# The last second product of a two-layer kernel: another order of its products, four sums on GpSimd, a bank put back with the earlier part, two outputs stored in pieces

## The chip, the core and the metric

The kernel runs on one core of a Trainium2 chip. The metric is the device time of one execution in microseconds (us). TensorE (PE) multiplies matrices into PSUM banks; VectorE (DVE) and ScalarE (ACT) take results out of PSUM; GpSimd (POOL) and SyncE (SP) issue most of the DMAs, GpSimd those that add to what lies in memory.

## The reference

```python
x: (16, 512, 768)   w1: (768, 3072)   b1: (3072,)   w2: (3072, 768)   # float32
y = np.matmul(x, w1) + b1
y = np.maximum(y, 0)
return np.matmul(y, w2).astype(np.float32)
```

## The kernel before

The 8192 rows are taken in eight blocks of 1024, the 3072 hidden columns in two chunks of 1536. An iteration is one block with one chunk, so there are 16: eight with the first chunk, then eight with the second. Each iteration has a first product (x by w1, bias and relu, into `y`) and a second (`y` by w2). The operands are fp16, the sums fp32.

**Fewer products.** Both products are cut into blocks and done by a fast scheme: sums of input blocks are formed on VectorE (for the second product the "y sums", L1046), fewer block products are done on TensorE (26 in the second product), and the outputs are formed from sums of products. The tables `SECOND_U`, `SECOND_V` (inputs of each product), `SECOND_CHAINS` and `SECOND_OPS` say how. A chain is a pair of PSUM banks: products ("m") are added into it one after another, and between them an operation ("t") reads the state of the bank pair. An operation gives an output (`out`, with the number of one of eight output blocks of 256 rows by 384 columns), a sum to keep (`sum`, in one of nine slots of `s`), or a value that seeds another chain's banks (`seed`). An operation without a kept sum as second input goes to ScalarE, one with such an input to VectorE (`operation`, L1219, through `combine`, L1207). One product is six matmuls of 128x384: two row halves (j = 0, 1), each over three parts of the hidden columns (`product`, L1196).

**The order of the work.** `SECOND_ORDER` and, for the last iteration, `LAST_ORDER` give the order of the products. All else is a graph of tasks: `Graph.add` records each task with its engine, an assumed duration, its inputs and outputs, and `Graph.run` plans the order of each engine's instructions and which bank or slot a task takes, by due times counted back from TensorE. The engines then run their instructions in that fixed order, each waiting on semaphores. SP and GpSimd issue the stores in their own planned order; an issue waits in its queue for its data, and those behind it wait too.

**The last iteration.** In the second chunk's other iterations GpSimd's stores (L1252, L1255) add the outputs to the first chunk's part, which lies in memory. In the last one, seven of the eight output blocks (`LAST_DIRECT`, all but operation 6) are done without that: SP loads the first chunk's part (`add_priors`, L1174) into places of `x` that are free by then, and it is added on the chip before a plain store from SP (L1250). `prior(to)` is that part of output `to`. Where the operation has a kept sum as well, `prior_task` first adds the kept sum to the part (L1260, x<-x,s, on VectorE since `LAST_POOL` is empty): for operations 0, 1, 3, 4, 5 and 7. Then one VectorE sum of bank and part (L1216) gives the output.

For operation 5 (`LAST_FOLD`) it is otherwise: its part is added into the bank pair on VectorE (`fold`, L1277) before the chain's last product, and ScalarE then copies the finished bank out (L1210). The last output (operation 1, output 3) is formed in two row halves on VectorE (`half`), stored from ACT's and SP's queues (`store_half`, L1245).

The last products are, in this order, 21, 11, 25, 23, 7, 16, 5, 6, 22, 9, 24, 20. Product 22 ends the chain of operation 10, which ScalarE writes, with the sign turned, into the bank pair of product 24; operation 0 (output 2) reads that after product 24. Product 9 leads to operation 5 (output 1), 20 to operation 1 (output 3), 6 to operation 3 (output 5), 5 to operation 2 (output 4), 16 to operation 4 (output 0), 25 to operation 7 (output 7). The kept sums that operations 0, 1, 3, 4, 5 need are those of operations 9, 14, 12, 11 and 20.

At the end of the program every engine loads a flag (L1387) that says whether the inputs were in range for the fast path, branches over the general path (L1512), and SP works off closing semaphores (L1540).

Of the kernel before, what the change touches and what calls it, by code (L numbers as in the profile page):

```python
# [87 lines left out]
SECOND_OPS = {  # L88
    0: (1, 1, 9, 1, 'out', 2, None),
    1: (4, 1, 14, 1, 'out', 3, None),  # L90
    2: (0, 1, None, None, 'out', 4, None),
    3: (4, -1, 12, 1, 'out', 5, None),
    4: (2, -1, 11, 1, 'out', 0, None),
    5: (2, 1, 20, 1, 'out', 1, None),
    6: (3, 1, 19, 1, 'out', 6, None),
    7: (5, 1, 16, 1, 'out', 7, None),
# [19 lines left out]
SECOND_CHAINS = ((('m', 5), ('t', 2)), (('m', 24), ('t', 0)), (('m', 13), ('t', 24), ('m', 4),  # L116
# [6 lines left out]
SECOND_SEEDS = (8, 10, None, 23, 24, 18, 13, None)  # L123
SECOND_ORDER = (13, 15, 4, 17, 10, 8, 12, 18, 3, 0, 1, 14, 2, 19, 23, 21, 11, 16, 25, 22, 7, 9, 6,
    24, 5, 20)
LAST_ORDER = (13, 15, 4, 17, 10, 8, 12, 18, 3, 0, 1, 14, 2, 19, 21, 11, 25, 23, 7, 16, 5, 6, 22,
    9, 24, 20)
LAST_FOLD = (5,)
LAST_DIRECT = (0, 1, 2, 3, 4, 5, 7)
LAST_POOL = ()  # L130

X_FUSE = (3,)
Y_FUSE = (8, 12, 18, 20)
# [453 lines left out]
class Fast:  # L587
# [590 lines left out]
    def add_second(self, it):  # L1178
        c = it // self.NSB
        nc = self.nc  # L1180
        final = it == self.NIT - 1
# [4 lines left out]
        bank, kept, done = {}, {}, 0  # L1186
        uses = [SECOND_OPS[t][2] for t in SECOND_OPS]
        NH, QM = self.NH, self.QM
        steps = sequence(SECOND_CHAINS, SECOND_SEEDS, SECOND_OPS, order)
        last = [n for k, n in steps if k == "t" and SECOND_OPS[n][4] == "out"][-1]  # L1190

        def pair(reg):
            a = reg.at[0]
            return self.ps[:, a:a + 2, 0:NH]

        def product(p, ch, start):  # L1196
            for j, h in ((j, h) for j in range(2) for h in range(3)):
                m0 = h * QM + j * P
                nc.tensor.matmul(self.ps[:, bank[ch].at[j], 0:NH],  # L1199
                                 lhsT=self.y[:, ys[SECOND_U[p]], m0:m0 + P],  # L1200
                                 rhs=self.v2[:, slot[SECOND_V[p]], h, :],
                                 start=(start and h == 0), stop=(h == 2), skip_group_check=True)
# [4 lines left out]
        def combine(engine, out, ps, a, s, b):  # L1207
            if s is None:
                if engine is nc.scalar:
                    nc.scalar.activation(out=out, in_=ps, func=ACTF.Copy, scale=float(a))  # L1210
                else:
                    engine.tensor_scalar(out=out, in0=ps, scalar1=float(a), scalar2=None,
                                         op0=ALU.mult)
                return
            in0, in1 = (ps, s) if a > 0 else (s, ps)
            engine.tensor_tensor(out=out, in0=in0, in1=in1,  # L1216
                                 op=ALU.add if a == b else ALU.subtract)
# [16 lines left out]
                combine(nc.scalar if alone else nc.vector, out, ps, a,  # L1234
                        None if alone else sum_of(kept[u]), b)

        def half(t, j, dest):
            ch, a, _, _, _, to, _ = SECOND_OPS[t]
            out = self.s[:, dest.at[0], 0:NH]
            combine(nc.scalar if t in folds and j == 0 else nc.vector, out, pair(bank[ch])[:, j],  # L1240
                    a, None if t in folds else self.prior(to)[:, j], 1)

        def store_half(to, j, dest):
            s = self.s[:, dest.at[0], 0:NH]
            (nc.scalar, nc.sync)[j].dma_start(out=self.rows_of(it, to)[:, j], in_=s)  # L1245

        def store(to, reg, plain):
            out, rows = sum_of(reg), self.rows_of(it, to)
# [14 lines left out]
        def prior_task(t):  # L1263
            _, _, u, b, _, to, _ = SECOND_OPS[t]
            e, ns = ("POOL", 1850) if t in LAST_POOL else ("DVE", 955)
            self.g.add(e, ns, lambda: add_prior(to, u, b, e),
                       reads=self.prior_keys(to) + [kept[u]], writes=self.prior_keys(to))
# [13 lines left out]

        where = {p: ch for ch, chain in enumerate(SECOND_CHAINS) for k, p in chain if k == "m"}
        folds = set()
        for kind, n in steps:
            if kind == "m":
                self.add_y_sums(order, done)
                done += 1
                ch = where[n]
                start = ch not in bank
                if start:  # L1290
                    bank[ch] = Reg("ps", 2, leaves=1)
                t = SECOND_CHAINS[ch][-1][1]
                if final and t in LAST_FOLD and t in LAST_DIRECT and not start and SECOND_CHAINS[ch][-2] == ("m", n):
                    fold(t)
                    folds.add(t)
                u, w = ys[SECOND_U[n]], slot[SECOND_V[n]]
                self.g.add("PE", 976, lambda p=n, ch=ch, start=start: product(p, ch, start),
                           reads=self.y_keys(u) + [("w2", w, h) for h in range(3)] +
                           ([] if start else [bank[ch]]), writes=[bank[ch]])
                continue  # L1300
            ch, a, u, b, what, to, _ = SECOND_OPS[n]
            reads = [bank[ch]]
            engine = "ACT" if u is None else "DVE"
            if u is not None:
                uses.remove(u)
            if what == "out":
                dest = Reg("s")
                direct = final and n in LAST_DIRECT
                if n in folds:
                    engine = "ACT"  # L1310
                elif direct:
                    engine = "DVE"
                    if u is not None:
                        prior_task(n)
                    reads += self.prior_keys(to)
                elif n in apart:
                    assert b == 1
                    self.g.add("POOL" if c else "SP", 1375 if c else 100,
                               lambda to=to, u=u: store_sum(to, u), reads=[kept[u]],
                               writes=[("out", self.block(it), to)], lat=9.0,  # L1320
                               dma=2.45 if c else 1.2)
                    engine = "ACT"
                elif u is not None:
                    reads.append(kept[u])
                    dest = dest if u in uses else kept[u]
            else:
                if u is not None:
                    reads.append(kept[u])
                if what == "sum":
                    dest = kept[n] = Reg("s") if u is None or u in uses else kept[u]  # L1330
                else:
                    dest = bank[to] = Reg("ps", 2, seeded=1, leaves=1)
            if what == "out" and final and n == last:
                for j in range(2):
                    dest = Reg("s")
                    e = "ACT" if n in folds and j == 0 else "DVE"
                    self.g.add(e, 500, lambda t=n, j=j, dest=dest: half(t, j, dest),
                               reads=reads, writes=[dest])
                    self.g.add(("ACT", "SP")[j], 100, lambda to=to, j=j, dest=dest: store_half(to, j, dest),
                               reads=[dest], writes=[("half", j)], lat=3.5, dma=0.6)  # L1340
                continue
            writes = [dest]
            split = engine == "ACT" and n in HALVES and n not in folds
            self.g.add(engine, 850 if split else 810 if engine == "ACT" else 955,
                       lambda t=n, dest=dest: operation(t, dest), reads=reads, writes=writes,
                       early=0.37 if split else 0)
            if what == "out":
                plain = c == 0 and n not in apart or direct
                self.g.add("SP" if plain else "POOL", 100 if plain else 1375,
                           lambda to=to, dest=dest, plain=plain: store(to, dest, plain),  # L1350
                           reads=[dest], writes=[("out", self.block(it), to)],
                           lat=3.5 if direct else 9.0, dma=1.2 if plain else 2.45)

# [189 lines left out]
```

## Time and profile before

| what | us |
|---|---|
| median of 3 runs (848.92 to 849.01) | 849.0 |
| span of the profiled execution, first to last instruction | 847.4 |
| TensorE busy | 839.4 |
| VectorE busy | 737.9 |
| ScalarE busy | 569.4 |
| GpSimd busy | 164.1 |

The median is the metric; the span belongs to one profiled execution, and the difference of 1.6 us lies around it. Durations in the prediction come from that execution. In a timeline row stand start, duration, engine, line, operation, output <- input, shape and count; a merged row gives the start of the first and the time to the end of the last. In a row of groups, after the bar, stand the busy time in us, the mean of one in ns, and after the next bar the engine's idle time before them with what ended it. "PEld" is TensorE's weight load; an engine's name with a q (SPq) is its queue, where it issues DMAs or works on semaphores. In rows of stretches the busy times of PE, PEld, DVE, ACT and POOL are followed by the granted clock of TensorE, the busy share of the DMA engines and their GB/s.

### The profile page before, as it was taken

To read this page: it belongs to the slowest core of one execution; us is meant where nothing else is said; L and a number is where in the kernel's file an instruction comes from. 1 tells how busy PE (TensorE), PEld (TensorE's weight loads), DVE (VectorE), ACT (ScalarE), POOL (GpSimd) and SP (SyncE) were. 2 spreads that over 40 slices of the span, in tenths; PEclk is the share of its full clock that TensorE was granted. 3 is DMA by queue.
4 is the path that set the end of the run, shared out by engine and by line. 5 is a ranking of instruction groups with operands and counts; after the bars stand their busy time and mean duration, and the time that the engine had idled before them with its cause. 6 is when DMAs were issued, how large, how long until landed. Compare 5 with 4: busy or idle time off the path is not lost. (4 is left out here: it accounts for less than half of the span.)

```text
span 847.4 us, 16784 instructions
## 1 busy us (share of the span) xinstructions
PE 839.4 (99%) x6381; PEld 625.5 (74%) x6381; DVE 737.9 (87%) x1231; ACT 569.4 (67%) x1203; POOL 164.1 (19%) x179
## 2 busy tenths in 40 slices
PE   8999999999999999999999999999999999999997
PEld 7558778686786867768687686877868678686874
DVE  5898987969889697998999979798896979979788
ACT  5866876778677695756858558766757666456463
POOL 5210011102111010010030503224041230501300
PEclk9999999999999999999999999999999999999999
DMA  9996497978988678594793977979789797985836
GB/s 213 202 180 176 81 233 105 163 183 133 222 113 148 169 126 192 95 223 150 224 187 65 192 123 124 187 106 178 125 128 150 116 173 113 147 134 75 146 117 169
DMA packets 170967, 128.93 MB, mean 152 GB/s; under 512 B 93804, under 2 KB 169348, under 8 KB 170884
## 3 DMA queue, kind: packets, MB, share of 16 engines
q0 software_dynamic: 56560, 68.82, 53.1%
q1 hardware_dynamic: 113856, 58.02, 28.3%
q8 instruction: 50, 0.82, 0.4%
q10 hardware_dynamic: 468, 1.00, 0.3%
q14 instruction: 33, 0.27, 0.1%
HBM read 73.54 MB, written 69.21 MB: 168 GB/s over the span
## 5 line engine op out<-in xcount | busy, mean ns | idle before, releaser
L1199 PE MATMUL ps<-v,y 128*128 128x384 f16 x2496 | 408.4, 326 | 0.0
L1073 PE MATMUL ps<-x,v 128*128 128x256 f16 x3600 | 395.7, 273 | 0.0
L1073 PEld LDWEIGHTS <-v 128*128 128x128 f16 x3600 | 352.2, 98 | 42.4 <-issue 0.2
L1199 PEld LDWEIGHTS <-y 128*128 128x128 f16 x2496 | 244.2, 98 | 160.0 <-issue 0.2
L1210 ACT ACTIVATE s<-ps 128x384 f32<-128x384 f32 (+1 forms) x244 | 153.0, 646 | 121.3 <-PE ps L1199 120.2
L1046 DVE TENSOR_TENSOR y<-y 128x768 f16<-128x768 f16 (+1 forms) x384 | 219.4, 619 | 2.6
L1116 DVE CUSTOM_DVE_ANT_0 y<-ps,s 128x512 f16<-128x512 f32 x240 | 156.0, 686 | 54.4 <-ACT s L1113 41.4
L1252 POOL DMA_DIRECT2D out_dram<-s x78 | 93.9, 1470 | 145.4 <-ACT s L1210 97.0
L1113 ACT ACTIVATE s<-ps,bt 128x256 f32<-128x256 f32 x180 | 75.3, 470 | 62.5 <-PE ps L1073 56.7
L828 DVE TENSOR_TENSOR x<-x 128x768 f16<-128x768 f16 (+1 forms) x210 | 113.7, 579 | 1.3
L1113 ACT ACTIVATE y<-ps,bt 128x256 f16<-128x256 f32 x180 | 69.5, 486 | 10.8 <-PE ps L1073 10.8
L1210 ACT ACTIVATE ps<-ps 128x384 f32<-128x384 f32 (+1 forms) x144 | 67.9, 509 | 8.1 <-PE ps L1199 6.6
L1216 DVE TENSOR_TENSOR s<-ps,s 128x768 f32<-128x768 f32 x74 | 70.5, 953 | 1.2 <-issue 0.3
L706 POOL DMA_DIRECT2D xn<-in_x_dram x30 | 25.9, 863 | 214.0 <-DMA x<-xn 99.5
L1216 DVE TENSOR_TENSOR s<-s,ps 128x768 f32<-128x768 f32 x60 | 57.1, 951 | 2.2 <-DVE s L1216 0.5
L767 ACT ACTIVATE junk<-xn 128x768 f16<-128x768 f16 x64 | 54.0, 843 | 0.3
L1255 POOL DMA_DIRECT2D out_dram<-s x15 | 17.7, 1181 | 169.5 <-ACT s L1210 157.7
L1113 ACT ACTIVATE ps<-ps,bt 128x256 f32<-128x256 f32 x60 | 26.7, 445 | 32.4 <-PE ps L1073 31.4
L1109 ACT ACTIVATE ps<-ps 128x512 f32<-128x512 f32 x60 | 35.3, 588 | 4.1 <-DVE y L1116 3.5
L1124 DVE TENSOR_TENSOR s<-s,ps 128x512 f32<-128x512 f32 x30 | 20.6, 688 | 17.7 <-PE ps L1073 17.7
L983 PE MATMUL ps<-x,v 128*128 128x256 f16 (+1 forms) x216 | 32.0, 308 | 0.7 <-DVE x L933 0.7
L1119 DVE SCALAR_TENSOR_TENSOR s<-ps,bt,s 128x256 f32<-128x256 f32 x60 | 26.1, 477 | 4.4 <-PE ps L1073 4.4
(60 smaller groups left out, 304.8 us busy)
## 6 DMA issues: line engine op xcount, KB each, us to landing
out_dram<-s POOLq DMA_DIRECT2D x93, 384.0 KB, 8.8
out_dram<-s SPq DMA_DIRECT2D x70, 384.0 KB, 6.6
xn<-in_x_dram POOLq DMA_DIRECT2D x28, 768.0 KB, 9.7
x<-out_dram SPq DMA_DIRECT2D x7, 384.0 KB, 3.5
v<-in_w_dram POOLq DMA_DIRECT2D x6, 384.0 KB, 10.6
v<-in_w_dram POOLq DMA_DIRECT2D x12, 192.0 KB, 9.1
w1d<-in_w_dram POOLq DMA_DIRECT2D x6, 384.0 KB, 6.5
w2d<-in_w_dram POOLq DMA_DIRECT2D x12, 192.0 KB, 4.9
```

Of the source, the lines that this page charges most:

```text
L767: self.nc.scalar.activation(out=self.junk, in_=self.xn[:, s, :], func=ACTF.Square, accum_out=self.stat[:, self.stat_at["x"] + i:][:, 0:1])
L828: self.nc.vector.tensor_tensor(out=self.two(x, out), in0=self.two(x, in0), in1=self.two(x, in1), op=ALU.add if sign > 0 else ALU.subtract)
L983: nc.tensor.matmul(self.ps[:, ps.at[0], cols], lhsT=self.v1[:, gi, 2 * h + k2, k, j * P:(j + 1) * P], rhs=rhs, start=(k2 == 0 and k == 0), ...
L1046: self.nc.vector.tensor_tensor(out=self.two(self.y, out), in0=self.two(self.y, in0), in1=self.two(self.y, in1), op=ALU.add if sign > 0 els ...
L1073: nc.tensor.matmul(self.ps[:, at, j * self.QM:(j + 1) * self.QM], lhsT=self.v1[:, gi, self.w1s[c][gi][FIRST_V[p]], k, j * P:(j + 1) * P], ...
L1109: nc.scalar.activation(out=out, in_=ps, scale=float(a), func=func if kind == "out" else ACTF.Copy)
L1113: nc.scalar.activation(out=out[:, j], in_=ps[:, j], func=func, scale=float(a), bias=beta(j))
L1116: nc.vector._custom_dve(TENSOR_ADD_SAT, out=out, in0=ps, in1=s, s0=F_MAX, s1=0.0)
L1199: nc.tensor.matmul(self.ps[:, bank[ch].at[j], 0:NH], lhsT=self.y[:, ys[SECOND_U[p]], m0:m0 + P], rhs=self.v2[:, slot[SECOND_V[p]], h, :], ...
L1210: nc.scalar.activation(out=out, in_=ps, func=ACTF.Copy, scale=float(a))
L1216: engine.tensor_tensor(out=out, in0=in0, in1=in1, op=ALU.add if a == b else ALU.subtract)
L1252: nc.gpsimd.dma_start(out=rows, in_=out, accum_op=ALU.add)
```

## The change

It touches the last iteration's second product alone.

- `LAST_ORDER` ends in 21, 11, 23, 25, 7, 16, 5, 6, 9, 22, 20, 24: product 23 comes ahead of 25, 9 ahead of 22, 20 ahead of 24.
- `LAST_POOL` puts the sum of kept sum and first chunk's part on GpSimd for operations 1, 3, 4 and 5. VectorE keeps those of operations 0 and 7. In GpSimd's order the one of operation 5 stands before the adding store of output 6, and those of operations 1, 4 and 3 (outputs 3, 0, 5) behind it.
- `LAST_FOLD` is empty: operation 5 is formed on VectorE from bank and part, as the others are.
- `LAST_TAKE`: the seed of operation 10 is written by VectorE in two row halves as part minus bank, with the first chunk's part (and kept sum) of output 2 already in it. Product 24, now the last, is added to that, so that its bank then holds the finished output 2.
- The last product is issued as two tasks, one for each row half.
- `LAST_PARTS`: output 2 goes out in three pieces: row half 0 (384 columns) copied by ScalarE and stored from SP; of row half 1 the first 192 columns by VectorE, stored from SP, and the rest by ScalarE, stored from ACT's queue.
- `LAST_HALVES`: output 3 (operation 1) is formed in two row halves on VectorE, both stored from SP.

```diff
-LAST_ORDER = (13, 15, 4, 17, 10, 8, 12, 18, 3, 0, 1, 14, 2, 19, 21, 11, 25, 23, 7, 16, 5, 6, 22,
-    9, 24, 20)
-LAST_FOLD = (5,)
+LAST_ORDER = (13, 15, 4, 17, 10, 8, 12, 18, 3, 0, 1, 14, 2, 19, 21, 11, 23, 25, 7, 16, 5, 6, 9,
+    22, 20, 24)
+LAST_FOLD = ()
+LAST_TAKE = {10: 0}
+LAST_HALVES = (1,)
+LAST_PARTS = ((0, 0, 384, "ACT", "SP"), (1, 0, 192, "DVE", "SP"), (1, 192, 384, "ACT", "ACT"))
 LAST_DIRECT = (0, 1, 2, 3, 4, 5, 7)
-LAST_POOL = ()
+LAST_POOL = (1, 3, 4, 5)
...
-        def product(p, ch, start):
-            for j, h in ((j, h) for j in range(2) for h in range(3)):
+        def product(p, ch, start, rows=(0, 1)):
+            for j, h in ((j, h) for j in rows for h in range(3)):
...
+        def part(t, j, cols, dest, e):
+            ch, a = SECOND_OPS[t][:2]
+            combine(nc.scalar if e == "ACT" else nc.vector, self.s[:, dest.at[0], cols],
+                    pair(bank[ch])[:, j, cols], a, None, None)
+
+        def store_part(to, j, cols, dest, e):
+            (nc.scalar if e == "ACT" else nc.sync).dma_start(
+                out=self.rows_of(it, to)[:, j, cols], in_=self.s[:, dest.at[0], cols])
...
+                if final and t == last and SECOND_CHAINS[ch][-2] == ("m", n):
+                    for j in range(2):
+                        self.g.add("PE", 488, lambda p=n, ch=ch, start=start, j=j:
+                                   product(p, ch, start, (j,)),
+                                   reads=self.y_keys(u) + [("w2", w, h) for h in range(3)] +
+                                   ([] if start else [bank[ch]]) +
+                                   ([("taken", t, j)] if t in taken_by else []),
+                                   writes=[("last", j)] + ([] if t in taken_by else [bank[ch]]))
+                    continue
...
             if what == "out" and final and n == last:
+                assert n in folds
+                for j, c0, c1, e, q in LAST_PARTS:
+                    dest = Reg("s")
+                    cols = slice(c0, c1)
+                    self.g.add(e, 100 + 1.05 * (c1 - c0),
+                               lambda t=n, j=j, cols=cols, dest=dest, e=e:
+                               part(t, j, cols, dest, e),
+                               reads=[("last", j)] + (reads if j else []), writes=[dest])
+                    self.g.add(q, 100, lambda to=to, j=j, cols=cols, dest=dest, q=q:
+                               store_part(to, j, cols, dest, q),
+                               reads=[dest], writes=[("part", j, c0)], lat=3.5, dma=0.545 * (c1 - c0) / 384)
+                continue
+            taken = LAST_TAKE.get(n) if final else None
+            if taken is not None:
...
+                folds.add(taken)
+                prior_task(taken)
+                of = SECOND_OPS[taken][5]
+                for j in range(2):
+                    self.g.add("DVE", 548, lambda ch=ch, a=a, of=of, dest=dest, j=j: combine(
+                        nc.vector, pair(dest)[:, j], pair(bank[ch])[:, j], a,
+                        self.prior(of)[:, j], 1),
+                        reads=reads + self.prior_keys(of) + ([dest] if j else []),
+                        writes=[("taken", taken, j)] + ([] if j else [dest]))
+                continue
+            if what == "out" and direct and n in LAST_HALVES:
...
                 for j in range(2):
                     dest = Reg("s")
+                    self.g.add("DVE", 548, lambda j=j, to=to, ch=ch, a=a, dest=dest: combine(
+                        nc.vector, self.s[:, dest.at[0], 0:NH], pair(bank[ch])[:, j], a,
+                        self.prior(to)[:, j], 1), reads=reads, writes=[dest])
+                    self.g.add("SP", 100, lambda to=to, j=j, dest=dest: store_part(
+                        to, j, slice(0, NH), dest, "SP"),
+                        reads=[dest], writes=[("half", to, j)], lat=3.5, dma=0.545)
                 continue
```

More of the change, by code (lines that the diff above doesn't have):

```diff
@@ L1235, in operation @@
                         None if alone else sum_of(kept[u]), b)
[L1237 to L1245, printed above, removed]
+        def part(t, j, cols, dest, e):
[5 more added lines that the diff above has]
+                out=self.rows_of(it, to)[:, j, cols], in_=self.s[:, dest.at[0], cols])
         def store(to, reg, plain):
@@ L1283, in add_second @@
         folds = set()
+        taken_by = set(LAST_TAKE.values()) if final else ()
         for kind, n in steps:
@@ new lines, in add_second @@
+                continue
+            taken = LAST_TAKE.get(n) if final else None
+            if taken is not None:
+                assert engine == "ACT" and what == "seed" and SECOND_OPS[taken][1] == 1
+                folds.add(taken)
[8 more added lines that the diff above has]
+                continue
@@ L1334, in add_second @@
+            if what == "out" and direct and n in LAST_HALVES:
+                assert n not in folds
                 for j in range(2):
                     dest = Reg("s")
[L1336 to L1340, printed above, removed]
+                    self.g.add("DVE", 548, lambda j=j, to=to, ch=ch, a=a, dest=dest: combine(
[4 more added lines that the diff above has]
+                        reads=[dest], writes=[("half", to, j)], lat=3.5, dma=0.545)
@@ L1351, in add_second @@
                            reads=[dest], writes=[("out", self.block(it), to)],
-                           lat=3.5 if direct else 9.0, dma=1.2 if plain else 2.45)
+                           lat=3.5 if direct else 9.0,
+                           dma=1.09 if direct else 1.2 if plain else 2.45)
     def add_check(self):
```

## The prediction

> **What bounds the kernel now.** I read the page's busy shares first, then the groups of the last second product (816.7 us to the end), then its timeline, then the DMA shares of the last 5 us, then SP's last issues.
>
> ```profile
> span 847.4 us, 16784 instructions
> PE 839.4 (99%) x6381; PEld 625.5 (74%) x6381; DVE 737.9 (87%) x1231; ACT 569.4 (67%) x1203; POOL 164.1 (19%) x179
> ```
>
> TensorE is busy 99% of the span, and the change leaves its matmuls as they are: 156 in this last product. So the change can gain only two things: TensorE's waits inside the last product, and the time from TensorE's last matmul to the end.
>
> ```profile
> 816.78 25.66 PE L1199 MATMUL ps<-v,y 128*128 128x384 f16 x156
> 832.47 9.59 PEld L1199 LDWEIGHTS <-y 128*128 128x128 f16 x59 [0.15 <-issue]
> 840.99 1.46 PE L1199 MATMUL ps<-v,y 128*128 128x384 f16 x8
> ```
>
> 156 matmuls in 25.66 us at 326 ns modelled for one start every 0.163 us; eight undisturbed ones start every (1.46 - 0.326)/7 = 0.162. So hardly more than 0.2 us of waiting exists here, and the weight loads show 0.15 of it at 832.47. One product (six matmuls) takes 0.98, and its bank is read about 0.2 after its slot ends. The last matmul ends at 816.78 + 25.66 = 842.44 by the model, so the last slot ends at 842.44 - 0.326 + 0.163 = 842.28.
>
> ```profile
> 837.44 0.96 DVE L1277 TENSOR_TENSOR ps<-ps,x 128x768 f32<-128x768 f32 x1
> 838.31 0.95 DVE L1216 TENSOR_TENSOR s<-ps,x 128x768 f32<-128x768 f32 x1
> 839.17 0.94 DVE L1216 TENSOR_TENSOR s<-x,ps 128x768 f32<-128x768 f32 x1
> 839.49 0.80 ACT L1210 ACTIVATE ps<-ps 128x768 f32<-128x768 f32 x1 [3.42 <-PE ps L1199]
> 840.03 1.82 DVE L1260 TENSOR_TENSOR x<-x,s 128x768 f32<-128x768 f32 x2
> 840.47 0.81 ACT L1210 ACTIVATE s<-ps 128x768 f32<-128x768 f32 x1 [0.18 <-PE ps L1199]
> 841.77 1.88 DVE L1216 TENSOR_TENSOR s<-ps,x 128x768 f32<-128x768 f32 x3
> 843.26 0.38 ACTq L1245 DMA_DIRECT2D out_dram<-s  x1
> 843.68 0.34 SPq L1245 DMA_DIRECT2D out_dram<-s  x1
> ```
>
> VectorE runs without a hole to 843.65: sums of 768 columns start 0.87 apart (837.44, 838.31, 839.17). Its last three (one whole output, two halves) could have started on the last bank at 842.28 + 0.2 = 842.48; the first half starts at 841.77 + 0.87 = 842.64, 0.16 late. So VectorE is only just the last engine. The last store is issued at 843.68, 0.03 after the last half.
>
> ```profile
> 844.50:845.00 0.50, 0.00 (x0) 0.00 (x0) 0.00 (x0) 0.00 (x0) 0.00 (x0) 1.00 1.06 378
> 845.00:845.50 0.50, 0.00 (x0) 0.00 (x0) 0.00 (x0) 0.00 (x0) 0.00 (x0) 0.72 1.01 360
> 845.50:846.00 0.50, 0.00 (x0) 0.00 (x0) 0.00 (x0) 0.00 (x0) 0.00 (x0) 0.50 0.72 250
> ```
>
> (the last columns are the share of the DMA engines' time and GB/s), and of the half stores, the flag's load and the closing instructions:
>
> ```profile
> DMA to landing us min/median/max: 2.5/2.6/2.6
> ...
> L1387 SPq TENSOR_LOAD <-flag x1: 973/973/973, 844.1 to 844.1; - x1
> ...
> L1540 SPq EVENT_SEMAPHORE  x14: 17/28/28, 845.4 to 847.4; - x14
> ```
>
> After that issue two things run side by side. The DMA engines are full (shares about 1) at some 365 GB/s until 845.9, and the last store lands at 843.68 + 2.6 = 846.3. SP, right behind its issue, loads the flag (844.1, 0.97 us) and works off the closing semaphores from 845.4 to 847.4. Either way the end stands 847.4 - 843.68 = 3.7 us behind **SP's last issue**. That issue is the quantity to forecast.
>
> **The change part by part.** The built instruction order shows nothing changed on any engine before this last product.
>
> *Order of products.* 23 goes ahead of 25, 9 ahead of 22, 20 ahead of 24. This spaces out a product and the seed put into its bank, so the waits seen above (0.15, of at most 0.2) should go. Taken: 0.15, so the last slot ends at 842.13. Bounds: 0.2 gained, or 0.15 kept because another bank is late.
>
> *VectorE.* Its removed work: four sums of the first chunk's part and the adding into a bank:
>
> ```profile
> L1260 DVE TENSOR_TENSOR x<-x,s 128x768 f32<-128x768 f32 x6 | 5.5, 951 | 0.0
> L1210 ACT ACTIVATE s<-ps 128x384 f32<-128x384 f32 x8 | 3.8, 495 | 3.3 <-PE ps L1199 3.3
> ...
> L1216 DVE TENSOR_TENSOR s<-ps,x 128x384 f32<-128x384 f32 x2 | 1.0, 548 | 0.0
> ```
>
> and from the whole run's groups the one small copy out of a bank:
>
> ```profile
> L1368 DVE COPY stat<-ps 128x56 f32<-128x56 f32 x1 | 0.2, 217 | 0.1
> ```
>
> That is 4 x 0.87 + 0.87 = 4.35 of issue time. Added: operation 5's output, 0.87 (ScalarE had it), the seed of operation 10 as two halves on VectorE at 0.55 instead of ScalarE's 0.80, and a copy of 192 columns, while operation 0's whole sum (0.87) goes. Two half sums stay, now operation 1's. The net relief is about 3 us, but most lies under TensorE's work; what counts is the chain behind the last products, counted back from 842.13:
>
> - product 9's slot ends 839.20, 22's 840.18, 20's 841.15, 24's first row half 841.64, its second 842.13.
> - VectorE: output 5 at 839.40; first seed half at 840.38 (22's end + 0.2) to 840.93, ahead of 24's start at 841.15; second, started 0.47 later, ends 841.40, ahead of 24's second half at 841.64 by 0.24. TensorE waits for neither.
> - output 3's halves start at 841.35 and 841.82, ending 841.90 and 842.37. Copy of 192 columns: between 0.217 (56 columns) and 0.548 (384), by a line 0.35; 842.33 to 842.68.
> - ScalarE: row 0 of output 2 (384 columns, 0.50) from 841.84 to 842.34; its 192 columns of row 1 to 842.7; then its own store issue.
>
> So engines finish at 842.7 against 843.65: 0.95 us earlier. But SP now issues four pieces there (two halves of output 3, row 0, the left of row 1), and they queue behind one another.
>
> ```profile
> 802.57 1.03 SPq L1174 DMA_DIRECT2D x<-out_dram  x2
> 412.84 0.32 SPq L1472 DMA_DIRECT2D v<-w2d  x1
> 413.26 0.45 SPq L1255 DMA_DIRECT2D out_dram<-s  x1
> ```
>
> No row shows two stores of this size with their waits already met. Bounds: 0.42 from issue to issue (412.84 to 413.26) and 0.65 (two loads of 0.37 in 1.03). I take 0.5, near the shorter, because a half store takes 0.34 where those loads took 0.37. Then SP issues at 841.93, 842.43, 842.93 and **843.43**, 0.25 ahead of 843.68. Three quarters of what the engines gain is given back in SP's queue; with 0.65 the last issue is 843.88, 0.2 later than before.
>
> *Bytes.* Outputs 3 and 2 are 0.79 MB as before, 2.15 us at 365 GB/s; the stretch from a store's issue to data is under 1 us, so they end by about 845.1, hidden under SP's closing 3.7 us. Were SP's chain shorter, this would be next.
>
> *GpSimd.* Three of its four sums (outputs 3, 0, 5) stand in a row behind operation 14, which ends at 831.8:
>
> ```profile
> 830.86 0.95 DVE L1216 TENSOR_TENSOR s<-s,ps 128x768 f32<-128x768 f32 x1
> ```
>
> and GpSimd's nearest rows are two casts:
>
> ```profile
> L1441 POOL CAST good<-y 1x1 f32<-1x1 f16 x5 | 0.9, 176 | 125.3 <-DVE y L1116 125.3
> ...
> L660 POOL CAST ident<-ident 128x128 f16<-128x128 f32 x1 | 0.3, 291 | 0.1
> ```
>
> No sum on GpSimd is in the trace. From its casts, (291 - 176)/127 = 0.9 ns a column: 0.87 us for 768 columns if both inputs come side by side, 1.56 if one after the other; the planner's code charges 1.85. I take 1.6, near the doubled cast, and keep 0.87 to 1.85. Then the third ends at 831.9 + 3 x 1.6 = 836.7 (1.85: 837.5). Operation 3 on VectorE waits for it; behind it in VectorE's queue stand output 5, the seed halves and everything above, and TensorE's last product waits for the seed. Counted back from 841.15: operation 3 must start by 841.15 - 0.2 - 0.55 - 2 x 0.87 = 838.66. So the cover is 1.1 to 1.9 us, and I cost GpSimd at nothing. The first sum (output 1) has over 8 us; GpSimd's accumulating store of output 6 stands behind it, and nothing in this tail waits for that but a buffer used at 841.
>
> **Sum.** Last issue 843.43 + 3.7 = 847.2 span, 0.25 under 847.4. The median 849.0 lies 1.6 over this profiled span, time outside it that I leave as it is; so 848.8. Less than a term's own doubt: near no change.
>
> **The rivals.**
>
> *VectorE and GpSimd take turns.* The trace has no GpSimd sum beside VectorE, so nothing in it excludes that these hold each other up. VectorE's operations that, as GpSimd's sums do, read both inputs from SBUF are the y sums (L1046) and the two part sums it keeps. Mechanism: the first GpSimd sum holds up the y sums by about 0.7 (1.6 less the 0.87 of a sum on PSUM beside it), which delays operation 14; GpSimd then waits out one part sum (0.87), VectorE's other one fits between GpSimd's second and third. About 2.3 us go into the chain: operation 3 starts at 831.9 + 2.3 + 3p + 0.1, against 838.66. With p = 1.6 TensorE waits 0.4, with 1.85 1.2; everything behind slips as much: 849.2 to 850.0, middle **849.6**.
>
> The Trainium skill states such a rule ("SBUF — State Buffer", Who interferes with whom): VectorE and GpSimd share one pair of SBUF ports as an exclusive lock, held for a whole instruction, and an operation with two SBUF inputs is among those that take it. No run shown here can show it. By that rule the time is this rival's. The Trainium skill's "GPSIMD Engine Reference" (Measured numbers in section 3.1) gives 1.96 times VectorE's time for such a sum; by 0.951 us that would be an estimated 1.86, and this rival 850.0.
>
> *SP's pieces 0.65 apart.* The new queue in place of VectorE's: last issue 843.88, time **849.2**.
>
> *SP off the end.* With issues 0.42 apart the last is 843.19; if the smaller last piece also lets the closing run shorten, **848.3**. Speaking for it: landing and closing lie within a few tenths now. Against: SP's closing run starts from its own queue.
>
> *GpSimd's sums too slow: slower.* One mechanism: three sums in a row keep operation 3, and so the last seed, waiting. It passes 0.2% (850.7, 1.9 us over my forecast) when p exceeds (838.56 + 1.9 - 831.9)/3 = 2.85 us alone, or 2.1 us with the turns above. At p = 2.3 with turns: 848.8 + (834.2 + 6.9 + 0.1 - 838.66) = **851.3**. Rows for GpSimd bound it lower, so it is small.
>
> *The tail does more than it says.* Past 0.2% faster (under 847.3) the last issue would have to come 1.7 us earlier, before TensorE's last slot ends; only a shorter closing run could give it.
>
> **How the numbers follow.** Forecast 848.8: 0.40. Turns 849.6: 0.30. SP 0.65 apart 849.2: 0.12. SP off the end 848.3: 0.10. GpSimd too slow 851.3: 0.06. More than 1.7 us faster: 0.02. The rest is noise among the near cases. The range takes the first four: from 848.2 (just under the fourth) to 850.0 (the turns with p at 1.85). 0.2% is 1.7 us, about what a measurement of this kernel tells from no change: under 847.3 faster 0.02, over 850.7 slower 0.06, between 0.92.
>
> **What would show it.** Order: the 0.15 at 832.47 gone and 156 matmuls in about 25.5 us. VectorE: no hole between operation 3 and the seed halves; holes "<-POOL" there speak for turns or slow sums, and y sums over 552 ns or GpSimd sums of varying length beside VectorE's for turns. GpSimd: four sums, each 0.87 to 1.85. SP: its last four issues 0.42 to 0.65 apart, the last near 843.4, the end 3.7 behind it. I am wrong if TensorE's last matmul ends later than 842.4, or if the end follows the landing instead of SP.

## The result, and the profile after

The changed kernel takes 850.1 us (median of 21 runs, 850.0 to 851.5) where the kernel before takes 848.9 on the same chip: ratio 1.0015, 95% interval 1.0009 to 1.0021. So it is 0.15% slower; forecast were 848.8 and a range to 850.0. The profiled executions lie up to 1.3 us apart after their first 41 us, in which the kernels do not differ, and a median of few runs can carry some of that. The first two lines of the page after:

```profile
span 848.6 us, 16793 instructions
...
PE 840.3 (99%) x6381; PEld 625.5 (74%) x6381; DVE 737.9 (87%) x1229; ACT 568.1 (67%) x1203; POOL 172.6 (20%) x183
```

The span grew by 1.1 us (848.56 after 847.45, before rounding). GpSimd has 8.5 us more work; VectorE's busy time has not fallen, 737.9 as before, although by the forecast's count some 3 us net were taken off it. Something else filled that time. The timeline of the last product after (line numbers of the changed kernel: y sums L1049, part sums L1262, matmuls L1202, sums of bank and part L1219, pieces L1246):

```profile
824.77 3.52 DVE L1049 TENSOR_TENSOR y<-y 128x768 f16<-128x768 f16 x2
825.26 2.21 POOL L1262 TENSOR_TENSOR x<-x,s 128x768 f32<-128x768 f32 x1
...
828.35 0.78 PEld L1202 LDWEIGHTS <-y 128*128 128x128 f16 x6 [0.19 <-DVE y L1049]
...
829.68 1.15 PE L1202 MATMUL ps<-v,y 128*128 128x384 f16 x6 [0.16 <-DVE y L1049]
...
831.01 7.97 PE L1202 MATMUL ps<-v,y 128*128 128x384 f16 x48 [0.18 <-DVE y L1049]
...
833.32 6.71 POOL L1262 TENSOR_TENSOR x<-x,s 128x768 f32<-128x768 f32 x3 [2.17 <-DVE s L1219]
...
834.02 0.94 DVE L1219 TENSOR_TENSOR s<-ps,s 128x768 f32<-128x768 f32 x1
...
836.05 2.30 DVE L1262 TENSOR_TENSOR x<-x,s 128x768 f32<-128x768 f32 x1
...
838.28 0.94 DVE L1219 TENSOR_TENSOR s<-x,ps 128x768 f32<-128x768 f32 x1
...
839.27 4.27 PE L1202 MATMUL ps<-v,y 128*128 128x384 f16 x24 [0.28 <-DVE s L1219]
...
841.80 1.02 DVE L1219 TENSOR_TENSOR ps<-x,ps 128x384 f32<-128x384 f32 x2
842.41 0.74 PEld L1202 LDWEIGHTS <-y 128*128 128x128 f16 x5 [0.28 <-issue]
...
843.35 1.84 SPq L1246 DMA_DIRECT2D out_dram<-s  x4
843.66 0.35 DVE L1215 TENSOR_SCALAR s<-ps 128x192 f32<-128x192 f32 x1
844.04 0.33 ACT L1213 ACTIVATE s<-ps 128x192 f32<-128x192 f32 x1 [0.41 <-DVE s L1215]
```

Read it in pairs. Two y sums that take 1.54 us undisturbed (experiment 1 has that row) take 3.52 beside GpSimd's first sum; VectorE's part sum at 836.05, 0.95 alone, takes 2.30 beside GpSimd's second and third of the row of three. These two stretches, 1.98 and 1.35 us, are what filled VectorE's time: the profile books its waiting here as busy time. The VectorE sum at 834.02, also beside a GpSimd sum but with one input in PSUM, keeps its 0.94. GpSimd's three sums take 6.71 where three undisturbed ones would take 5.4 (1.80 each, experiment 6).

TensorE then waits where it had hardly waited: twice for a y sum, then at 839.27 for the bank that operation 4 had not yet read (the sum at 838.28, behind the stretched part sum), then at 842.41 for the seed (the first of the two halves at 841.80). From matmul start to matmul start these gaps are 0.49, 0.51, 0.61 and 0.38 us instead of 0.163: 0.33 + 0.35 + 0.45 + 0.21 = 1.33 in all, 0.16 before. The last matmul starts at 843.22, 1.09 later than before (842.12), and SP's last issue comes at 844.79, 1.11 later (843.68). From there to the end:

```profile
L1581 SPq EVENT_SEMAPHORE  x14: 17/28/28, 846.6 to 848.5; - x14
```

SP works off its closing semaphores from 846.6 to 848.5, and the end stands 3.8 us behind its last issue, as before. So the whole loss is made inside the product, by TensorE's four waits.

### The profile page after: what moved, and what is told of

Its sections match the earlier page's. It is cut to its first block, busy times and chain, and to the rows that moved or that the text cites. A ratio compares the mean times of both kernels' runs of the same rounds, so it can differ in the third digit from the quotient of the medians.

```text
span 848.6 us, 16793 instructions
## 1 busy us (share of the span) xinstructions
PE 840.3 (99%) x6381; PEld 625.5 (74%) x6381; DVE 737.9 (87%) x1229; ACT 568.1 (67%) x1203; POOL 172.6 (20%) x183
## 5 line engine op out<-in xcount | busy, mean ns | idle before, releaser
L1202 PE MATMUL ps<-v,y 128*128 128x384 f16 x2496 | 408.9, 326 | 0.7 <-DVE y L1049 0.3
L1202 PEld LDWEIGHTS <-y 128*128 128x128 f16 x2496 | 243.9, 98 | 161.5 <-DVE y L1049 1.3
L1213 ACT ACTIVATE s<-ps 128x384 f32<-128x384 f32 (+2 forms) x245 | 152.9, 643 | 127.1 <-PE ps L1202 125.7
L1049 DVE TENSOR_TENSOR y<-y 128x768 f16<-128x768 f16 (+1 forms) x384 | 221.3, 624 | 2.6
L1219 DVE TENSOR_TENSOR s<-ps,s 128x768 f32<-128x768 f32 x74 | 70.6, 953 | 1.2 <-issue 0.4
L1219 DVE TENSOR_TENSOR s<-s,ps 128x768 f32<-128x768 f32 x60 | 57.1, 951 | 2.2 <-DVE s L1219 0.5
```

The lines of the kernel that those rows point to most:

```text
L1049: self.nc.vector.tensor_tensor(out=self.two(self.y, out), in0=self.two(self.y, in0), in1=self.two(self.y, in1), op=ALU.add if sign > 0 els ...
L1202: nc.tensor.matmul(self.ps[:, bank[ch].at[j], 0:NH], lhsT=self.y[:, ys[SECOND_U[p]], m0:m0 + P], rhs=self.v2[:, slot[SECOND_V[p]], h, :], ...
L1219: engine.tensor_tensor(out=out, in0=in0, in1=in1, op=ALU.add if a == b else ALU.subtract)
```

## The experiments

Theory A: GpSimd's and VectorE's sums take turns, whenever both have both inputs in SBUF; the stretched VectorE sums make TensorE wait. Theory B: GpSimd's sums are simply slow, and operation 3 and the seed wait for them. Theory C: the new order, the put-back seed or the pieces cost the time. Each run is compared with the kernel before on its own chip (849.15, 849.26, 849.17 and 848.94 us in the four sessions). In brackets stand the ratio of the runs and its 95% interval; it is not formed from the two medians alone.

**1. All part sums on VectorE.** From the changed kernel:

```diff
-LAST_POOL = (1, 3, 4, 5)
+LAST_POOL = ()
```

> The changed kernel with all part sums back on VectorE. Both theories: the two waits of TensorE for y sums (0.33 and 0.35 us in the changed kernel's trace) are gone. VectorE has four sums (3.5 us) more ahead of the seed halves; counted from before's timeline, where operation 0 began at 841.77, the first seed half begins there and the last product starts at about 842.5 instead of 841.2: 849.8 to 850.2. If instead the seed halves or the pieces were what cost the time, and not GpSimd, it is 850.1 with all of the changed kernel's waits still there.

851.5 against 849.15 (1.0025, 1.0014 to 1.0036), above the 849.8 to 850.2 expected. Rows of its timeline and two stretches of half a us (last columns: clock, share of the DMA engines, GB/s):

```profile
824.87 1.54 DVE L1049 TENSOR_TENSOR y<-y 128x768 f16<-128x768 f16 x2
...
836.75 5.04 PE L1202 MATMUL ps<-v,y 128*128 128x384 f16 x30 [0.31 <-ACT ps L1213]
...
842.12 1.14 PE L1202 MATMUL ps<-v,y 128*128 128x384 f16 x6 [0.33 <-DVE ps L1219]
...
843.88 2.40 SPq L1246 DMA_DIRECT2D out_dram<-s  x4
```

```profile
843.00:843.50 0.50, 0.25 (x2) 0.00 (x0) 0.50 (x2) 0.50 (x2) 0.00 (x0) 1.00 0.00 0
...
846.50:847.00 0.50, 0.00 (x0) 0.00 (x0) 0.00 (x0) 0.00 (x0) 0.00 (x0) 0.50 1.06 379
```

With GpSimd's sums gone, both waits for y sums are gone and the y sums last 1.54 again: that much of A holds. The time is still worse. VectorE now does two part sums in a row at 839.8, so three outputs come out together behind 843.4: the DMA engines idle until then and are full behind it. TensorE has two other waits, 0.47 us at 836.75 and 0.49 at 842.12 (from start to start, beyond the usual). Without sums on GpSimd the changed order leaves VectorE too late.

**2. Only the GpSimd sums, in the kernel before.** Nothing else changed:

```diff
-LAST_POOL = ()
+LAST_POOL = (1, 3, 4, 5)
```

> The kernel before with nothing changed but the four sums on GpSimd. Turns (GpSimd's sum and a VectorE operation with two SBUF inputs keep each other out): TensorE waits about 0.7 us for y sums at 829 to 831 and again for operation 4's bank, 849.6 to 850.2, and y sums beside a GpSimd sum last over 2 us. Slow sums only (GpSimd's sum is long, and only what needs its result waits): output 1's sum has 8 us of cover, VectorE is relieved of 3.5 us: 848.6 to 848.9, every y sum at 0.55 or 0.95.

850.6 against 849.15 (1.002, 1.0011 to 1.0029): 0.4 above the upper end of A's 849.6 to 850.2, and far from B's 848.6 to 848.9. Its timeline (y sums L1046, part sums L1260):

```profile
824.85 3.53 DVE L1046 TENSOR_TENSOR y<-y 128x768 f16<-128x768 f16 x2
825.35 2.21 POOL L1260 TENSOR_TENSOR x<-x,s 128x768 f32<-128x768 f32 x1
...
833.41 6.70 POOL L1260 TENSOR_TENSOR x<-x,s 128x768 f32<-128x768 f32 x3 [1.72 <-DVE s L1216]
835.84 2.60 DVE L1260 TENSOR_TENSOR x<-x,s 128x768 f32<-128x768 f32 x1
```

The same four stretched rows, without the new order, the put-back or the pieces. The sums on GpSimd alone bring the whole loss, and C falls as its main cause.

**3. No GpSimd sum for operation 5,** the one beside the y sums:

```diff
-LAST_POOL = (1, 3, 4, 5)
+LAST_POOL = (1, 3, 4)
```

> The changed kernel with operation 5's sum back on VectorE, three left on GpSimd; the first GpSimd sum, the one beside the y sums, is gone. Turns: the 0.67 us of waits for y sums go, the later ones stay: 849.3 to 849.6. Slow sums only: that sum had 8 us of cover and cost nothing, so 850.1, or more by VectorE's extra sum.

851.0 against 849.15 (1.002, 1.001 to 1.0029): far above A's 849.3 to 849.6. B had named 850.1 "or more", so the number alone would not speak against it. Its timeline:

```profile
831.70 3.43 DVE L1262 TENSOR_TENSOR x<-x,s 128x768 f32<-128x768 f32 x2
831.87 6.70 POOL L1262 TENSOR_TENSOR x<-x,s 128x768 f32<-128x768 f32 x3
...
836.78 2.60 DVE L1262 TENSOR_TENSOR x<-x,s 128x768 f32<-128x768 f32 x1
...
837.48 2.11 PE L1202 MATMUL ps<-v,y 128*128 128x384 f16 x12 [0.84 <-ACT ps L1213]
```

The waits for y sums went, as A has it, but the sum given back to VectorE now stands beside GpSimd's other three and is stretched itself. The collision moved to a worse place: A had the mechanism and missed where it would strike next.

**4. Sums that nobody needs.** Experiment 1's kernel, all part sums on VectorE, plus four GpSimd sums of the same size on an unused buffer; no engine waits for them. It adds work and leaves none out.

```diff
+    def add_idle_sums(self, count, at):
...
+                self.nc.gpsimd.tensor_tensor(out=b, in0=a, in1=a, op=ALU.add)
```

> e1 with four sums on GpSimd at the places of the changed kernel's, on SBUF that nothing uses any more, so that no instruction waits for their results: what is left of GpSimd's cost is contention alone. Turns: 0.5 to 1.5 us over e1, with a y sum and a part sum of VectorE stretched past 2 us. Slow sums only: as e1 within 0.1 us, all VectorE sums at their usual length. It adds work and leaves none out.

859.4, 7.8 over experiment 1. Of this 1.3 us had come up by 41 us after the start in the profiled execution, before anything differs; 6.4 arise in the last product. Its timeline, and two stretches:

```profile
832.11 6.48 DVE L1049 TENSOR_TENSOR y<-y 128x768 f16<-128x768 f16 x4
832.30 5.40 POOL L1406 TENSOR_TENSOR v<-v 128x768 f32<-128x768 f32 x3
...
834.70 7.71 PE L1202 MATMUL ps<-v,y 128*128 128x384 f16 x36 [2.17 <-DVE y L1049]
```

```profile
835.70:839.10 3.40, 3.40 (x12) 1.60 (x11) 3.40 (x4) 1.20 (x2) 1.93 (x2) 0.51 0.06 10
839.10:842.00 2.90, 2.90 (x19) 1.79 (x18) 2.90 (x4) 0.59 (x2) 0.00 (x0) 0.99 0.00 0
```

B has no way to a loss here, since nobody waits for these sums: A's collision is shown by itself. In the changed kernel too B has next to nothing to explain: GpSimd's third sum ended at 840.03, and operation 3, which needs it, started at 840.06, 0.92 us after the sum ahead of it on VectorE instead of 0.87. So B falls. Four y sums that take 1.96 us in experiment 1 take 6.48. The size was missed by far (0.5 to 1.5 expected): more y sums were hit than I had counted, and the granted clock fell to 0.51 for 3.4 us, of which below.

**5. Writing without reading.** The same with a `memset` of 1536 columns in place of each idle sum of 768, so that GpSimd is busy about as long:

```diff
-                self.nc.gpsimd.tensor_tensor(out=b, in0=a, in1=a, op=ALU.add)
+                self.nc.gpsimd.memset(a, 0.0)
```

> As e4 with memsets of 1536 columns (about 1.8 us by the row of the 128-column memset) in place of the four idle sums: GpSimd works as long and writes SBUF, but reads nothing. If it is the reading of SBUF that VectorE's two-input operations wait for: as e1, 2.4 us over before, no VectorE sum stretched. If any GpSimd work holds them up: as e4, several us over e1. It adds work and leaves none out.

851.7, 2.4 over its kernel before, as experiment 1 was (2.4). Its timeline:

```profile
825.64 1.54 DVE L1049 TENSOR_TENSOR y<-y 128x768 f16<-128x768 f16 x2
826.03 1.86 POOL L1405 MEMSET v<- 128x1536 f32 x1
...
831.51 4.74 POOL L1405 MEMSET v<- 128x1536 f32 x3
832.28 1.90 DVE L1262 TENSOR_TENSOR x<-x,s 128x768 f32<-128x768 f32 x2
```

GpSimd is about as busy beside them as before (1.86 us, and 1.58 each for the three), and the two y sums keep their 1.54, the two part sums 1.90. It isn't GpSimd's activity but its reading of SBUF that excludes them. The Trainium skill says so ("SBUF — State Buffer", Who interferes with whom): a VectorE instruction with two SBUF inputs contends with a GpSimd instruction that reads SBUF, not with one that only writes it; the runs agree, down to the 0.94 of a sum with one input in PSUM.

**6. GpSimd's sums behind VectorE's.** The kernel before with two sums (operations 0 and 1) on GpSimd, held back by one-element copies that wait for VectorE's last part sum:

```diff
-LAST_POOL = ()
+LAST_POOL = (0, 1)
+LAST_GATE = (0, 5)
...
+                for n in LAST_GATE:
+                    self.g.add("POOL", 180, lambda n=n: nc.gpsimd.tensor_copy(
+                        out=self.good[0:1], in_=self.prior(n)[0:1, 0, 0:1]),
+                        reads=self.prior_keys(n), writes=["mark"])
```

> The kernel before with two sums on GpSimd (outputs 2 and 3) that begin only when VectorE's last operation with two SBUF inputs is done (two one-element copies on GpSimd wait for it); after that VectorE reads one input from PSUM in all it does. Turns: nothing is stretched on either engine (GpSimd's sums about 1.8 us, VectorE's 0.95), no new wait of TensorE, and VectorE's backlog at the end (0.16 us) goes: 0.1 to 0.2 us under before. If any GpSimd sum slows any VectorE operation: VectorE's 0.95 become longer from 837 on and the time is above before.

849.06 against 849.26 (1.0, 0.9991 to 1.0009). Its timeline:

```profile
832.42 9.59 PEld L1200 LDWEIGHTS <-y 128*128 128x128 f16 x59 [0.15 <-issue]
...
836.83 3.59 POOL L1261 TENSOR_TENSOR x<-x,s 128x768 f32<-128x768 f32 x2
...
843.47 0.34 SPq L1246 DMA_DIRECT2D out_dram<-s  x1
```

Two GpSimd sums in 3.59 us, 1.80 each, and no loss. The same instruction that lasts up to 2.5 us in a collision, and stretches VectorE's, costs nothing measurable a quarter of a us behind VectorE's last part sum.

**7. The changed kernel with that gate.** Order, put-back and pieces as changed; `LAST_POOL = (0, 1)`, `LAST_GATE = (0, 5, 1)`, the copies as in 6.

> The changed kernel with GpSimd's sums cut to two (operations 0 and 1), begun only after VectorE's last operation with two SBUF inputs. Turns: TensorE's four waits shrink to the one before the last product (0.2 us at most), and what is left of the change is its seed halves and the four pieces in SP's queue: last SP issue near 843.7, so 0.1 over before to 0.1 under, 1 us or more under the changed kernel. If the seed halves and pieces are what cost: as the changed kernel.

849.19 against 849.26 (1.0001, 0.9992 to 1.001). Its timeline:

```profile
836.78 5.62 PEld L1203 LDWEIGHTS <-y 128*128 128x128 f16 x35 [0.27 <-issue]
...
837.53 3.58 POOL L1263 TENSOR_TENSOR x<-x,s 128x768 f32<-128x768 f32 x2
...
842.33 2.04 SPq L1247 DMA_DIRECT2D out_dram<-s  x4
```

With two sums instead of four on GpSimd, and none of them in a collision, the loss is gone; that fewer sums alone don't do it, experiment 3 shows with its three. What is left of the change is worth nothing measurable either way. One wait of TensorE stays (0.27 in the row, 0.20 beyond the usual start), in another place than the old one.

**8. The changed kernel again,** unaltered, beside experiment 9.

> The changed kernel unaltered, beside the gated one on one chip. The theory that GpSimd's and VectorE's sums take turns expects 1.0 to 1.4 us over the kernel before of the same chip (TensorE's waits of 1.33 us against 0.16, carried to SyncE's last issue), with a y sum of about 2.9 us at 825 us and a part sum of about 2.3 us at 836 us again. If the earlier difference was a difference between executions, it comes out within 0.3 us of the kernel before.

850.43 against 849.17 (1.0014, 1.0005 to 1.0023), 1.25 over the gated kernel of experiment 9; the lowest runs of the two are 850.03 and 848.70. Its timeline, here 1.3 us later from 41 us after the start on:

```profile
826.06 3.52 DVE L1049 TENSOR_TENSOR y<-y 128x768 f16<-128x768 f16 x2
826.55 2.21 POOL L1262 TENSOR_TENSOR x<-x,s 128x768 f32<-128x768 f32 x1
...
837.35 2.30 DVE L1262 TENSOR_TENSOR x<-x,s 128x768 f32<-128x768 f32 x1
```

The stretched rows return to the hundredth.

**9. One piece less** at the end of the gated kernel:

```diff
-LAST_PARTS = ((0, 0, 384, "ACT", "SP"), (1, 0, 192, "DVE", "SP"), (1, 192, 384, "ACT", "ACT"))
+LAST_PARTS = ((0, 0, 384, "ACT", "ACT"), (1, 0, 384, "DVE", "SP"))
```

> The gated version (VectorE's y sums and part sums of two seeds end before GpSimd begins its two sums) with the second-last output in two pieces of 768 and the last as one store instead of more pieces. If SyncE's queue of issues ends the gated version (its four issues were 0.41, 0.67 and 0.55 us apart, the last at 943.94 less 100, that is 843.94), one issue less ends it at about 843.3 and the time is 0.3 to 0.5 us under the kernel before of the same chip. If the landing of the last bytes ends it, as in the kernel with the put-back alone, the time is within 0.2 us of the gated version's and no more than 0.2 under the kernel before.

849.18 against 849.17 (0.9999, 0.999 to 1.0008). SP's last issue came at 843.34, 0.6 earlier than in 7, and the end at 848.0, no earlier. Here the end is not 3.7 but 4.7 behind the last issue. SP's waits show why (us in total, times, longest):

```profile
SPq L1589 <- DMA out_dram<-s: 0.8, 1, 0.8
```

In its closing run SP waits 0.8 us for a store. The last one lands at 846.60, and SP goes on at 846.61: the landing, and not SP's own run, sets the end.

**10. Gate and a second put-back.** Experiment 6 with `LAST_FOLD = (5, 1)`: output 3's part is added into the bank early as well (and the due time of operation 2's task set to 835).

> e5, and output 3 put into its bank ahead of the last product, as the kernel before does with output 1, so that after the last product its two halves only have to be copied, by ScalarE and VectorE at once. Counted from before's rows: both copies start at 842.5 and end at 843.0 to 843.05, the last issue comes 0.6 us earlier than 843.68: 0.4 to 0.6 us under before. If SP's closing run does not start from its last issue, less.

849.05 against 849.26 (0.9995, 0.9986 to 1.0004): within 0.2, where 0.4 to 0.6 was expected. The last issue came at 843.04, 0.65 earlier than before; the end only 0.1 earlier. The landing of its last two half stores:

```profile
DMA to landing us min/median/max: 2.9/3.1/3.3
```

The last store lands 3.3 us after its issue (843.04 + 3.3 = 846.3); before, 2.6. Here too SP waits for it. What the engines gained, the landing gave back.

**11 and 12. Fewer bytes.** 10 and 9 with outputs 1 and 5 storing only their first row half; 0.39 MB of the last block is left out, all issues stay.

```diff
+            if final and to in LAST_CUT:
+                nc.sync.dma_start(out=rows[:, 0], in_=out[:, 0])
```

> The kernel with the gate and the put-back, but outputs 1 and 5 store only their first row half (0.39 MB of the last block's output is left out; the second row half of these outputs keeps the first chunk's part). The issues, their order and every engine's work stay. In the uncut kernel the last store was issued at 843.04 and landed 3.3 us later, where the stores that found the DMA engines free landed 2.45 after their issue; the end came 0.97 after that landing. If the end follows the landing of a backlog of bytes, the last store now lands at about 845.5, the end comes at 846.5, 0.8 earlier, and the time is 0.7 to 1.0 us under the kernel before of the same chip. If the end follows SyncE's issues and its closing run from its own queue, as the forecast had it, nothing changes: within 0.2 us of the kernel before.

> The gated changed kernel with two pieces for output 2, outputs 1 and 5 storing only their first row half as well (0.39 MB left out). Uncut, its last store was issued at 843.34 and landed 3.26 us later, the end 1.4 after that. By the backlog of bytes it now lands at about 845.8, the end comes at 847.2, 0.8 earlier, and the time is 0.6 to 0.9 us under the kernel before of the same chip. By SyncE's issues alone nothing changes: within 0.2 us of the kernel before.

11: 848.90 against 848.94, nothing gained. 12: 848.37 against 848.94 (0.9993, 0.9984 to 1.0002), end 1.0 earlier than in 9. In 11 the DMAs of the cut stores, then of the last two half stores, and the stretches:

```profile
DMA to landing us min/median/max: 1.9/1.9/1.9
```

```profile
DMA to landing us min/median/max: 2.8/3.0/3.3
```

```profile
843.00:843.50 0.50, 0.00 (x0) 0.00 (x0) 0.06 (x1) 0.00 (x0) 0.00 (x0) 1.00 0.00 0
843.50:844.00 0.50, 0.00 (x0) 0.00 (x0) 0.00 (x0) 0.00 (x0) 0.00 (x0) 1.00 0.97 350
...
845.50:846.00 0.50, 0.00 (x0) 0.00 (x0) 0.00 (x0) 0.00 (x0) 0.00 (x0) 1.00 0.43 155
```

In 11 no backlog is left (share 0.00 at 843.0) and the last store still lands 3.3 late. A half store that finds the engines free lands in 1.9, a whole one (before) in 2.5: 0.6 per half, and some 1.3 at both sizes. The put-back makes the last two outputs come at the same moment, 842.6: 842.6 + 1.3 + 4 x 0.55 = 846.1, measured 846.4. So there it is the bytes of the last two outputs that end the kernel, not those ahead of them; my backlog theory was wrong for 11. In 12 the last outputs come staggered, the backlog was what held them, and with it gone the half stores land as this row has it (uncut, the row reads 2.5/2.9/3.3):

```profile
DMA to landing us min/median/max: 1.9/2.2/2.4
```

The end comes 0.98 us behind the last landing in 10 and 11, and 1.41 in 9 and 12. In its closing run SP waits for the semaphores of the DMAs in a fixed order, one about every 0.06 us when they have landed; in 10 and 11 the last store's is the last of these waits, in 9 and 12 seven more follow it.

No kernel that computes the whole beat the kernel before by more than its interval; the best, 10, is 0.05% under it, with an interval that holds 1.

## Why the prediction was wrong, step by step

- **The failed step: GpSimd.** "So the cover is 1.1 to 1.9 us, and I cost GpSimd at nothing." The cover was counted for GpSimd's sums alone, and its own duration was not the error's core: undisturbed it is 1.80, inside 0.87 to 1.85. What I put at nothing was what GpSimd does to VectorE. Experiment 2 shows that it costs 1.5 us by itself, experiments 4 and 5 that reading is what collides, and 7 that without it the change is at 849.2. The term was worth 1.2 to 1.5 us. The cover went with it: operation 14, held up with the y sums, let GpSimd begin its three sums at 833.32 instead of 831.9, and they ended at 840.03 instead of 837.5.
- **The rival "VectorE and GpSimd take turns"** was the right one, with 0.30 where it should have been the likeliest: its mechanism, a y sum and a part sum, came as told, and its upper sum, 850.0, lies 0.1 under the measured 850.1. That closeness is partly luck. The sum takes 1.85 for one GpSimd sum; with the 1.80 that experiment 6 measured it gives 831.9 + 2.3 + 5.4 + 0.1 - 838.66 = 1.04 over 848.8, that is 849.8. The factor in the Trainium skill's "GPSIMD Engine Reference" (section 3.1) had given an estimated 1.86, a little above that measured 1.80. And the rival's path was only half right. I let the loss reach TensorE through operation 3 and the last seed; of the 1.33 us measured, 0.68 are direct waits for y sums, 0.45 is operation 4's bank, and only 0.21 the seed. The range ended at this rival's sum without room for that. The sign "y sums over 552 ns" was set too low: y sums of 1536 columns take 0.96 undisturbed.
- **Order: "Taken: 0.15".** The old wait went, but in the gated kernel 0.20 appears ahead of 836.78. That is the bound I named, "0.15 kept because another bank is late"; nothing was gained.
- **SP's pieces, 0.5 apart.** Right: 843.35, 843.77, 844.29, 844.79, that is 0.42, 0.51 and 0.50. The copy of 192 columns took 0.35, as estimated.
- **"The end stands 3.7 us behind SP's last issue".** The number came (3.8), but as a law it is wrong: 4.3 in experiment 10, 4.7 in 9. In the kernel before SP passed its wait for the last store at 846.49, 0.19 behind the landing, so its own run set the end. In the changed kernel the last piece landed at 847.23 and SP passed the wait for it at 847.25, so both came together, and that it was 3.8 again is partly chance. In experiments 1, 3 to 5, 7 and 9 to 12 the landing set the end. With that both signs of being wrong that the prediction names have come: in those runs the end follows the landing, and in the changed kernel the last matmul ended at 843.5 (843.22 + 0.326) instead of by 842.4. The step *Bytes*, which put the stores' end at 845.1 from "under 1 us" to data, was too low: the last landing was at 847.2, and at 846.3 even in the kernel before, as the prediction itself had read. The fixed part of a store is 1.3 us, and several outputs stand in the queue. Even without the collision the 0.25 us forecast as gain was not to be had: 0.07 in experiment 7, within its interval.

Not settled: why one of SP's last four issues in experiment 1 took 0.82 us (the others 0.44 to 0.46). Experiment 12's span is 1.0 shorter than experiment 9's, and its median 0.8 (848.37 and 849.18); it is only 0.57 under the kernel before because that kernel was itself 0.23 lower in 12's session.

## What to carry to other kernels

As far as these runs show, an elementwise sum with its inputs in SBUF is moved to GpSimd only where VectorE has, for its whole length, no operation with both inputs in SBUF; look at what stands beside it on VectorE before you look at its own duration, since the price is paid by VectorE and by those who wait for it. A gate that puts such sums behind VectorE's made two of them free. At the end of a kernel compute three bounds, not one: the issuing queue's closing run, the last issue plus a store's fixed part, and the bytes of all outputs that come together. Where a landing sets the end, look also at how many closing waits follow the one for that store.

## What the runs showed of the hardware that was not expected

- A collision costs VectorE nearly the whole rest of GpSimd's instruction and then its own: the y sum that began at 825.36 beside a GpSimd sum ending at 827.47 ended at 828.29, 0.82 later, for a sum of 0.96. The part sum that began at 836.05 beside one ending at 837.54 ended at 838.35, 0.81 later.
- In experiment 4 the granted clock fell to 0.51 for 3.4 us, one us after TensorE had resumed from a wait of 2.17 us; shortly before that two starts of matmuls had come 0.39 and 0.51 us after the ones ahead of them instead of 0.163. A wait of 2.13 us later in that run left the clock alone: 30 matmuls in 5.04 us, one each 0.163.

```profile
844.53 5.04 PE L1202 MATMUL ps<-v,y 128*128 128x384 f16 x30 [2.13 <-ACT ps L1213]
```

The Trainium skill ("TensorE: Matmul & The Clock Gate", Why this matters for your kernels) advises no idle gaps over about 3 us between bursts; here the clock fell after one of 2.17 and not after one of 2.13. What else it takes, no run here shows.
